# A held weight cast, a sum that starts in PSUM, and the last 384 columns scaled by TensorE: a change to a decoder layer on one core

## The chip, the core and the metric

The kernel runs on one core of a Trainium2 chip. The metric is device time in microseconds (us) of one execution, of which the profiled execution's span is the part between the first and the last recorded instruction.

Engines: PE is TensorE (matrix products), PEld its weight loads, DVE is VectorE, ACT is ScalarE, POOL is GpSimd, SP is SyncE, which here issues nearly all transfers.

## The reference

One decoder layer over 256 tokens of width 1024, batch 1, in float32:

```
z = h @ w_in;  u, q, k, v = split(z)                    # 512 columns each
pool = ((window mean of u) - u) @ w_pool[g] * pool_scale # windows 2, 4, 8, 16, one group of 128 each
attn = softmax(causal(q k^T / 8)) v                     # 8 heads of 64, one block of 256
h = LN1(alpha h + concat(pool, attn) @ w_out)
h = LN2(alpha h + cross_attention(h, mem) @ w_xo)       # 4 heads of 256, 256 memory tokens
h = LN3(alpha h + (silu(h w_gate) * (h w_up)) @ w_down) # d_ff = 2816
```

LN is (x - mean) / sqrt(var + eps) * g + b over the 1024 columns. alpha is 2 to the power 1/4.

## The kernel before

**Precision.** [...] So each operand is split into a high part (a cast by ScalarE) and a low part (the difference, by VectorE), and a product is three: high by high, high by low, low by high (`three`, L325 to L329). Operands that are left plain float32 (`f32`) go through TensorE in two slow passes: the transposes' data, the attention products and the pooled ones (`mix_pool`, L584).

**Weights.** All weights come in one stream (`Stream`, L49 on) of numbered tiles w0 to w130: a raw tile loaded by SP (w26r), then its cast (w26h, L157, ScalarE) and its subtraction (w26l, L159, VectorE). `prepare(upto)` issues casts and subtractions up to a tile, in program order on both engines, and lets SP load on as raw buffers come free (7 of them). Products ask for weights with `get`, which prepares what is needed and, unless `held` is set, one tile more at every `pace`-th call (L175). Instructions stand on each engine in the order in which the program issues them; there is no other scheduler.

**The stretch around the third pair.** After the q, k, v and u projections, the keys of the memory are projected (`xk`, L345, 32 steps of six products, at a pace of 3), and between its steps stand the pieces of the self-attention and the pooling. For each pair of heads, `probs_t(hp)` transposes the probabilities on TensorE into two PSUM banks pt (L543 to L545) and copies them to SBUF: the larger one on VectorE (sb, L548), the smaller on ScalarE (L549). `mix_pool(g)` multiplies the pooled group g by its matrix into a bank pm (L584), and splits the result (L585 ScalarE, L586 VectorE). `pool_diff(g)` (L580, VectorE) makes the input of mix_pool from GpSimd's window sums (L573, L576). Four PSUM banks go around among pt, pm and po (the attention product, L560 and L561); each has to be read out before it is written again. The order is: 12 steps of xk, probs_t(2), mix_pool(0), 8 steps, probs_t(3), mix_pool(1), pool_diff(2), 8 steps, attend(2), mix_pool(2), and so on (L634 on).

**The end.** The down projection of the FFN accumulates the two halves of tokens (t = 0, 1) in eight PSUM banks m; its last six weight tiles (w125 to w130) are multiplied piece by piece (`pieces`, L1034): 512 columns three times, then 256 twice. The very last piece, columns 768 to 1024 of t = 1, has its own bank (acc). Before that, what the other banks hold is joined with the residual in SBUF (r, L1074 to L1084; L1069 adds a bank to r). Each finished piece is added to r (L1069) and measured (L674, bn_stats). Then `finish` runs: aggregate (L679), variance plus eps (L681), power -1/2 on GpSimd (rs, L682), centring, which is (r - mean) * g (L687), scaling, which is r * rs + b (L692), and stores (L991). For t = 0 the scaling is done by ScalarE and GpSimd (L698, L699); for t = 1 it is done by VectorE in pieces of 512, 256 and 256 columns, each stored as soon as it is there.

Of the kernel before, what the change touches and what calls it, by code (L numbers as in the profile page):

```python
# [8 lines left out]
F32 = mybir.dt.float32  # L9
F32R = mybir.dt.float32r  # L10
AF = mybir.ActivationFunctionType
# [3 lines left out]
P = 128  # L15
D = 1024
# [3 lines left out]
CW = 256  # L20
# [13 lines left out]
PR_BUFS = 6  # L34
# [3 lines left out]
DOWN = (1, 0, 2, 3, 4, 7, 5, 6, 8, 9, 10)  # L38
SEVEN = (1, 2, 3, 4, 5, 6)
LAST = DOWN[-3:]  # L40


def r32(t):
    return t.bitcast(F32)


class Stream:
# [115 lines left out]
    def next(self):  # L163

        if not self.held:
            self.prepare(min(self.used + AHEAD, len(self.tiles) + 1))
# [27 lines left out]
def decoder_layer(  # L194
# [17 lines left out]
    def bank(name):  # L212
        return pb.tile([P, 512], F32, tag="b", name=name)

    def accbank(name):
        return pa.tile([P, 512], F32, tag="acc", name=name)


    ws = Stream(nc, wp)
# [70 lines left out]
    gb = {}  # L290
# [14 lines left out]

    ident = cp.tile([P, P], F32, name="ident")
    make_identity(nc, ident)
    tri = ep.tile([P, S], F32, name="tri")
    nc.gpsimd.memset(tri, 0.0)
    nc.gpsimd.affine_select(  # L310
# [13 lines left out]
    def three(ps, w, y, start, stop, part=False):  # L324

        (wa, wb), (ya, yb) = w, y
        nc.tensor.matmul(ps, wa, ya, start=start, stop=False, skip_group_check=part)  # L327
        nc.tensor.matmul(ps, wa, yb, start=False, stop=False, skip_group_check=part)  # L328
        nc.tensor.matmul(ps, wb, ya, start=False, stop=stop, skip_group_check=part)  # L329

    def pair(hl, *ix):
        return hl[0][ix], hl[1][ix]
# [48 lines left out]
    def run(gen, n=None):  # L381

        while n is None or n > 0:
            if next(gen, gen) is gen:
                return False
            n = None if n is None else n - 1
        return True

    def split(h, l, ps):
        nc.scalar.copy(h, ps)  # L390
        nc.vector.tensor_sub(l, ps, r32(h))  # L391
# [146 lines left out]
    def probs_t(hp):  # L538
        p0 = bank("pt0").rearrange("p (j t) -> p j t", j=2)
        p1 = bank("pt1")[:, :S].rearrange("p (j t) -> p j t", j=2)  # L540
        for j in range(2):
            q0, q1 = probs[hp // 2, 0, j][:, hp % 2], probs[hp // 2, 1, j][:, hp % 2]
            nc.tensor.transpose(p0[:, j, :P], q0[:, :P], ident)  # L543
            nc.tensor.transpose(p0[:, j, P:], q1[:, :P], ident)
            nc.tensor.transpose(p1[:, j, :], q1[:, P:], ident)  # L545
        sb = sp.tile([P, 2, 512], F32, name="sb", tag="pair", bufs=3)
        s0, s1 = sb[:, :, :S], sb[:, :, S:S + P]
        nc.vector.tensor_copy(s0, p0)  # L548
        nc.scalar.copy(s1, p1)  # L549
        pts[hp] = s0, s1  # L550
# [31 lines left out]
    def mix_pool(g):  # L582
        pm = bank("pm")
        nc.tensor.matmul(pm[:, :S], pool_w[:, g * P:(g + 1) * P], upad[:, g, PADW:], start=True, stop=True)  # L584
        nc.scalar.activation(cT[0][:, g, :], pm[:, :S], AF.Copy, bias=0.0, scale=psc[:, g:g + 1])  # L585
        nc.vector.scalar_tensor_tensor(cT[1][:, g, :], pm[:, :S], psc[:, g:g + 1],  # L586
                                       r32(cT[0][:, g, :]), op0=OP.mult, op1=OP.subtract)


    def do_v():  # L590
        pieces = [(t, 0, 512) for t in range(T)]
        acc = {piece: accbank("pv") for piece in pieces}
        yield from proj_rows(acc, c_v, lambda k: (xT[0][:, k], xT[1][:, k]), pieces, True, True, True)
        for piece in pieces:
            nc.scalar.copy(vt[:, piece[0], :], acc[piece])

    def do_u():
        for c in range(2):
            ps = accbank("pu").rearrange("p (f t) -> p f t", f=2)
# [6 lines left out]
    def do_xk():  # L606
        for c in range(4):
            ps = accbank("pxk").rearrange("p (f t) -> p f t", f=2)
            yield from proj_t([ps[:, f, :] for f in range(2)], c_xk[c], mT)
            split(xkT[0][:, 2 * c:2 * c + 2, :], xkT[1][:, 2 * c:2 * c + 2, :], ps)  # L610

    v, u, xk = do_v(), do_u(), do_xk()
# [18 lines left out]
    pool_diff(0)  # L631
    pool_diff(1)
    run(u)
    run(xk, 12)  # L634
    probs_t(2)
    mix_pool(0)
    run(xk, 8)
    probs_t(3)
    mix_pool(1)
# [17 lines left out]
    class Norm:  # L657
# [7 lines left out]
        def add(self, c0, c1, acc):  # L665
            self.sum(c0, c1, acc)
            self.measure(c0, c1)
# [2 lines left out]
            s = slice(c0, c1)  # L670
            nc.vector.scalar_tensor_tensor(self.r[:, s], self.tok[:, s], ALPHA, acc, op0=OP.mult, op1=OP.add)

        def measure(self, c0, c1):
            nc.vector.bn_stats(self.st[:, self.n, :], self.r[:, c0:c1])  # L674
            self.n += 1

        def stats(self):
# [3 lines left out]
            nc.vector.tensor_scalar(self.rs, self.mv[:, 1:2], EPS, None, op0=OP.add)  # L681
            nc.gpsimd.tensor_tensor(self.rs, self.rs, mhalf, op=OP.pow)  # L682

        def centre(self, c0, c1):
            s = slice(c0, c1)
            r = self.r[:, s]
            nc.vector.scalar_tensor_tensor(r, r, self.mv[:, 0:1], gb["g", self.i][:, s],  # L687
                                           op0=OP.subtract, op1=OP.mult)

        def scale(self, c0, c1):  # L690
# [10 lines left out]
        def finish(self):  # L701
            self.stats()
            for half in HALVES:
                self.centre(*half)
            for half in HALVES:
                self.scale(*half)

    HALVES = ((0, 512), (512, D))
# [22 lines left out]
    def until(gen):  # L731

        for got in gen:
            if got is not None:
                return got
# [6 lines left out]
    for t in range(T):  # L742
        norm = Norm(1, xt[:, t, :], h1[:, t, :])
# [123 lines left out]
    norm = Norm(2, h1[:, 0, :], h2[:, 0, :])  # L867
# [3 lines left out]
    norm = Norm(2, h1[:, 1, :], h2[:, 1, :])  # L871
# [29 lines left out]
    def gated_pair(c, k, t):  # L901

        return pair(gT[c], ALL, 2 * k + t)
# [86 lines left out]
    def store(t, y, c0, c1, queue=nc.sync):  # L990
        queue.dma_start(out[t * P:(t + 1) * P, c0:c1], y[:, c0:c1])  # L991
# [5 lines left out]
    def into(n, y, w, cols=ALL, ps=None):  # L997

        three((m[n] if ps is None else ps)[:, cols], y, w, n not in begun, True, True)
        begun.add(n)  # L1000
# [32 lines left out]

    def pieces():  # L1034

        for n, c0, c1 in ((2, 0, 512), (3, 0, 512), (4, 0, 512), (0, 0, 256), (0, 256, 512)):
            t, first, _ = QUARTERS[n]
            ps = accbank("acc") if c0 else m[n]
            for c in LAST:
                for k, number in enumerate(c_dn[c]):  # L1040
                    ws.prepare(number + 1)
                    w = pair(ws.tiles[number], ALL, 0, slice(first + c0, first + c1))
                    if c0:
                        three(ps[:, :c1 - c0], gated_pair(c, k, t), w, (c, k) == (LAST[0], 0), True, True)
                    else:
                        into(n, gated_pair(c, k, t), w, slice(c0, c1))
                    yield
            yield ps[:, :c1 - c0] if c0 else ps

    def down():  # L1050
        for c in DOWN[:-len(LAST)]:
            yield from (seven if c in SEVEN else eight)(c)

    dn = down()
# [8 lines left out]
    norms = [Norm(3, h2[:, t, :]) for t in range(T)]  # L1063

    def with_residual(t, s, y):
        nc.vector.scalar_tensor_tensor(norms[t].r[:, s], h2[:, t, s], ALPHA, y, op0=OP.mult, op1=OP.add)
# [15 lines left out]
    nc.vector.tensor_add(norms[1].r[:, upper], norms[1].r[:, upper], u3)  # L1082
    with_residual(1, lower, u3)
    add(norms[1], 768, D, m[0][:, 256:])  # L1084
    dn = pieces()

    def finish(norm, t):

        norm.stats()
        for half in HALVES:  # L1090
            norm.centre(*half)
        if t == 0:
            for half in HALVES:
                norm.scale_apart(*half)
            store(t, norm.r, 0, D)
            return
        for c0, c1, queue in ((0, 512, nc.sync), (512, 768, nc.scalar), (768, D, nc.sync)):
            norm.scale(c0, c1)
            store(t, norm.r, c0, c1, queue)

    norm = norms[0]
    for half in HALVES:
        add(norm, *half, until(dn))
        norm.measure(*half)
    finish(norm, 0)

    norm = norms[1]
    add(norm, *HALVES[0], until(dn))
    norm.measure(*HALVES[0])
    add(norm, 512, 768, until(dn)[:, :256])  # L1110
    norm.measure(512, 768)
    add(norm, 768, D, until(dn))
    norm.measure(768, D)
    finish(norm, 1)
    run(dn)


# [46 lines left out]
```

## Time and profile before

| | us |
|---|---|
| median of 3 runs | 379.49 (379.37 to 379.83) |
| profiled execution | 379.23 |
| its span | 377.5 |
| TensorE busy in the span | 368.3 |
| VectorE, ScalarE, GpSimd busy | 302.3, 201.3, 20.2 |

The lines quoted below come from the profile's page and from views of the trace. A timeline row gives start, duration, engine, source line, operation, output <- inputs, partitions x elements with types, how many; in brackets, how long the engine had been idle and which engine's operation ended that. A row of waits gives engine and operation, what it waited for, us in total, how often, and the longest. A group's row gives busy us and the mean ns of one behind the first bar. A transfer's row ends with its size and the us from issue to landing. A row of windows gives the stretch and its length, each engine's busy us, the granted TensorE clock (1.00 is full), the transfer share and GB/s. A row of the chain gives start, us and what. [...]

### The profile page before, as it was taken

How to read it: one execution, taken by the hardware profiler on the slowest of the kernel's cores; microseconds unless marked ns; L12 is line 12 of the kernel's file. 1: busy time of each engine (PE TensorE's matmuls, PEld its weight loads, DVE VectorE, ACT ScalarE, POOL GpSimd, SP SyncE). 2: the span in 40 equal slices, each digit the busy share in tenths (PEclk: the TensorE clock that was granted, in tenths of full speed). 3: DMA queues.
4: the chain of work that ended last, by engine and by line, in shares of the span. 5: the costliest groups of instructions: out<-in, count | busy, mean ns of one | idle time of the engine just before them, and what ended most of it. 6: DMA issues, size and time to landing. Idle time of an engine off the chain costs nothing.

```text
span 377.5 us, 5729 instructions
## 1 busy us (share of the span) xinstructions
PE 368.3 (98%) x2154; PEld 323.3 (86%) x2154; DVE 302.3 (80%) x470; ACT 201.3 (53%) x318; POOL 20.2 (5%) x27
## 2 busy tenths in 40 slices
PE   9999999899999999999999999999999999999992
PEld 8997989798888889998888888888888888888882
DVE  6868889955499687774899687788876998999995
ACT  5746668543253544644237575556666466466510
POOL 1000036100020000000100000000000000000022
PEclk9999999999999999999999999999999999999997
DMA  7997773658606964343206854666555863363102
GB/s 282 412 413 259 219 281 115 220 171 283 214 6 236 411 203 143 123 128 121 87 0 226 310 186 175 220 222 198 168 175 163 302 224 112 109 206 132 56 2 111
DMA packets 20892, 71.95 MB, mean 191 GB/s; under 512 B 2304, under 2 KB 3072, under 8 KB 20736
## 3 DMA queue, kind: packets, MB, share of 16 engines
q1 hardware_dynamic: 20432, 71.18, 54.3%
q8 instruction: 17, 0.28, 0.3%
q10 hardware_dynamic: 432, 0.39, 0.3%
q14 instruction: 11, 0.09, 0.1%
HBM read 70.52 MB, written 1.05 MB: 190 GB/s over the span
## 4 chain that ended last, share of the span: by engine, by line
PE 93%; DVE 2%; issue 2%; ACT 1%; DVEq 0%; ACTq 0%
PE pg L780 19%; PE pg L786 10%; PE pqk L461 6%; PE m L328 5%; PE m L329 5%; PE m L327 5%; PE pxk L345 4%; PE acc L327 4%; PE acc L328 4%; PE acc L329 4%; PE pxq L780 4%; PE pxq L786 2%; PE xv L327 2%; PE xv L329 2%; PE xv L328 2%
## 5 line engine op out<-in xcount | busy, mean ns | idle before, releaser
L682 POOL TENSOR_TENSOR rs<-rs,mhalf 128x1 f32<-128x1 f32 x6 | 5.4, 892 | 296.2 <-DVE rs L681 296.2
L390 ACT CAST g<-sg 128x512 fp32r<-128x512 f32 x12 | 7.4, 621 | 15.1 <-DVE sg L954 10.1
L391 DVE TENSOR_TENSOR g<-sg,g 128x512 fp32r<-128x512 f32 x12 | 8.3, 693 | 8.2 <-ACT g L390 8.2
L935 DVE TENSOR_TENSOR sg<-pg,sg 128x256 f32<-128x256 f32 x40 | 14.1, 416 | 0.0
L934 ACT COPY sg<-pg 128x256 f32<-128x256 f32 x40 | 12.0, 386 | 3.5 <-PE pg L786 3.3
L939 ACT ACTIVATE sg<-sg 128x512 f32<-128x512 f32 x10 | 6.4, 635 | 13.8 <-DVE sg L935 13.8
L497 ACT ACTIVATE xpr<-xs,mx 128x256 f32<-128x256 f32 x8 | 3.7, 468 | 14.3 <-DVE mx L508 14.3
L497 ACT ACTIVATE pr<-pr,mx 128x128 f32<-128x128 f32 (+1 forms) x16 | 7.1, 444 | 7.2 <-DVE mx L528 7.2
L390 ACT CAST h2T<-tp 128x512 fp32r<-128x512 f32 x4 | 2.3, 587 | 13.0 <-PE tp L418 12.9
L674 DVE BATCH_NORM_STATS2 st<-r 128x6 f32<-128x512 f32 (+1 forms) x13 | 8.5, 654 | 0.5
L687 DVE SCALAR_TENSOR_TENSOR r<-r,mv,g 128x512 f32<-128x512 f32 x12 | 8.5, 743 | 0.0
L940 DVE TENSOR_TENSOR sg<-sg 128x512 f32<-128x512 f32 x10 | 6.9, 692 | 0.9
L698 ACT ACTIVATE r<-r,rs 128x512 f32<-128x512 f32 x2 | 1.3, 716 | 11.4 <-POOL rs L682 11.4
L502 DVE RECIPROCAL sm<-sm 128x2 f32<-128x2 f32 x12 | 2.0, 166 | 6.0 <-ACT xpr L497 4.5
L812 PE MATMUL xs<-xkTh,xq 128*128 128x256 f32 x32 | 6.4, 282 | 0.0
L390 ACT CAST h1T<-tp 128x512 fp32r<-128x512 f32 x4 | 2.3, 587 | 7.1 <-PE tp L418 7.1
L573 POOL TENSOR_TENSOR win<-upad 128x542 f32<-128x542 f32 x2 | 3.2, 1596 | 54.4 <-ACT upad L601 54.4
L692 DVE SCALAR_TENSOR_TENSOR h<-r,rs,b 128x512 f32<-128x512 f32 x8 | 5.7, 747 | 0.1
L812 PEld LDWEIGHTS xs<-xkTh,xq 128*128 128x128 f32 x32 | 5.2, 191 | 0.2
L573 POOL TENSOR_TENSOR win<-win 128x269 f32<-128x269 f32 (+3 forms) x4 | 5.2, 1307 | 0.2
L157 ACT CAST w39h<-w39r 128x1024 fp32r<-128x1024 f32 x1 | 1.1, 1060 | 7.8 <-PE acc L329 7.8
L390 ACT CAST xkTh<-pxk 128x512 fp32r<-128x512 f32 x4 | 2.4, 588 | 4.9 <-PE pxk L345 4.9
(1169 smaller groups left out, 1376.7 us busy)
## 6 DMA issues: line engine op xcount, KB each, us to landing
g<-in_ln_g SPq DMA_DIRECT2D x3, 512.0 KB, 5.8
b<-in_ln_b SPq DMA_DIRECT2D x3, 512.0 KB, 6.8
wr<-in_w_qkv SPq DMA_DIRECT2D x5, 256.0 KB, 4.0
mr<-in_mem_t SPq DMA_DIRECT2D x1, 1024.0 KB, 11.3
xt<-in_x SPq DMA_DIRECT2D x1, 1024.0 KB, 8.5
xr<-in_x_t SPq DMA_DIRECT2D x3, 256.0 KB, 6.4
wr<-in_w_qkv SPq DMA_DIRECT2D x1, 512.0 KB, 6.2
w7r<-in_w_qkv SPq DMA_DIRECT2D x1, 512.0 KB, 7.2
```

The source lines that it names most:

```text
L327: nc.tensor.matmul(ps, wa, ya, start=start, stop=False, skip_group_check=part)
L328: nc.tensor.matmul(ps, wa, yb, start=False, stop=False, skip_group_check=part)
L329: nc.tensor.matmul(ps, wb, ya, start=False, stop=stop, skip_group_check=part)
L345: nc.tensor.matmul(pss[f], w[:, s], y, start=k == 0 and f == 0 and n == 0, stop=k == KD - 1 and n == 2, skip_group_check=True)
L390: nc.scalar.copy(h, ps)
L461: nc.tensor.matmul(qk[i][:, f, :], w[:, c * P:(c + 1) * P], y, start=k == 0 and f == 0 and w is hi and y is x_hi, stop=k == KD - 1 and w i ...
L497: nc.scalar.activation(dst[:, j, :], src[:, j, :], AF.Exp, bias=mx[:, j:j + 1], scale=sign, accum_out=sm[:, j:j + 1])
L780: nc.tensor.matmul(ps, hi[:, b * P:(b + 1) * P], yT.both(k), start=k == 0, stop=False, skip_group_check=True)
L786: nc.tensor.matmul(ps[:, S:], lo[:, b * P:(b + 1) * P], yT.pair(k)[0], start=False, stop=k == KD - 1, skip_group_check=True)
L812: nc.tensor.matmul(ps[:, t, :], q[:, kk, t * P:(t + 1) * P], k[:, 2 * h + kk], start=n == 0, stop=q is q_lo and kk == 1, skip_group_check= ...
L934: nc.scalar.copy(y[:, f, :], ps[:, S:])
L935: nc.vector.tensor_add(y[:, f, :], ps[:, :S], y[:, f, :])
```

## The change

Three edits, with a copy of the identity matrix in fp32r (ident_r) made at the start by VectorE.

1. After 7 of the 12 steps of xk ahead of the third pair's probs_t(2), the stream is held: no weight is prepared ahead until probs_t(2) and mix_pool(0) have been issued.
2. The last piece (columns 768 to 1024 of t = 1) does not begin with zero. What r already holds there is split into a high and a low part (rest), and two products with ident_r put it into the bank acc first. The addition afterwards goes; statistics and centring read acc directly.
3. Of the last norm's scaling, columns 640 to 1024 are done by TensorE: a product of the identity with b (128x384, float32), then one of a diagonal matrix of rs (made by ScalarE) with the centred r, summed in a bank, which ScalarE copies to SBUF and stores. VectorE scales columns 0 to 512 and 512 to 640. The centring goes in the order 768 to 1024, 640 to 768, 0 to 640. The stores are 512 columns (SP), 384 (ScalarE's queue) and 128 (SP), instead of 512, 256, 256.

```
+CUT = 640
...
+    ident_r = cp.tile([P, P], F32R, name="ident_r")
+    nc.vector.tensor_copy(ident_r, ident)
...
-    run(xk, 12)
+    run(xk, 7)
+    ws.held = True
+    run(xk, 5)
     probs_t(2)
     mix_pool(0)
+    ws.held = False
     run(xk, 8)
...
-        def measure(self, c0, c1):
-            nc.vector.bn_stats(self.st[:, self.n, :], self.r[:, c0:c1])
+        def measure(self, c0, c1, src=None):
+            nc.vector.bn_stats(self.st[:, self.n, :], self.r[:, c0:c1] if src is None else src)
...
-            nc.vector.scalar_tensor_tensor(r, r, self.mv[:, 0:1], gb["g", self.i][:, s],
+            nc.vector.scalar_tensor_tensor(r, r if src is None else src, self.mv[:, 0:1], gb["g", self.i][:, s],
...
             ps = accbank("acc") if c0 else m[n]
+            for part in rest if c0 else ():
+                nc.tensor.matmul(ps[:, :c1 - c0], ident_r, part, start=part is rest[0], stop=False,
+                                 skip_group_check=True)
...
-                        three(ps[:, :c1 - c0], gated_pair(c, k, t), w, (c, k) == (LAST[0], 0), True, True)
+                        three(ps[:, :c1 - c0], gated_pair(c, k, t), w, False, True, True)
...
     add(norms[1], 768, D, m[0][:, 256:])
+    rest = [sp.tile([P, CW], F32R, name=f"rest{i}", tag="pr", bufs=PR_BUFS) for i in range(2)]
+    split(*rest, norms[1].r[:, 768:])
     dn = pieces()
...
-    add(norm, 768, D, until(dn))
-    norm.measure(768, D)
-    finish(norm, 1)
+    acc = until(dn)
+    norm.measure(768, D, acc)
+    norm.stats()
+    norm.centre(768, D, acc)
+    norm.centre(CUT, 768)
+    norm.centre(0, CUT)
+    diag = sp.tile([P, P], F32, name="diag", tag="pr", bufs=PR_BUFS)
+    nc.scalar.activation(diag, ident, AF.Copy, bias=0.0, scale=norm.rs)
+    ps = bank("end")[:, :D - CUT]
+    nc.tensor.matmul(ps, ident, gb["b", 3][:, CUT:], start=True, stop=False)
+    nc.tensor.matmul(ps, diag, norm.r[:, CUT:], start=False, stop=True)
+    norm.scale(0, 512)
+    store(1, norm.r, 0, 512)
+    nc.scalar.copy(norm.r[:, CUT:], ps)
+    store(1, norm.r, CUT, D, nc.scalar)
+    norm.scale(512, CUT)
+    store(1, norm.r, 512, CUT)
     run(dn)
```

On each engine's list of instructions the first edit moves one weight: w26's cast goes from ahead of the smaller copy of probs_t(2) to behind the xk cast, and its subtraction from ahead of the copy sb to behind the xk subtraction; w27 to w30 each follow one place later, and from w31 on the lists agree again up to the end.

More of the change, by code (lines that the diff above doesn't have):

```diff
@@ L682, in stats, with centre @@
             nc.gpsimd.tensor_tensor(self.rs, self.rs, mhalf, op=OP.pow)
-        def centre(self, c0, c1):
+        def centre(self, c0, c1, src=None):
             s = slice(c0, c1)
             r = self.r[:, s]
-            nc.vector.scalar_tensor_tensor(r, r, self.mv[:, 0:1], gb["g", self.i][:, s],
+            nc.vector.scalar_tensor_tensor(r, r if src is None else src, self.mv[:, 0:1], gb["g", self.i][:, s],
                                            op0=OP.subtract, op1=OP.mult)
@@ L1084, in decoder_layer @@
     add(norms[1], 768, D, m[0][:, 256:])
+    rest = [sp.tile([P, CW], F32R, name=f"rest{i}", tag="pr", bufs=PR_BUFS) for i in range(2)]
+    split(*rest, norms[1].r[:, 768:])
     dn = pieces()
[L1087 to L1099, printed above, removed]
     norm = norms[0]
@@ L1104, in decoder_layer @@
         norm.measure(*half)
-    finish(norm, 0)
+    norm.stats()
+    for half in HALVES:
+        norm.centre(*half)
+    for half in HALVES:
+        norm.scale_apart(*half)
+    store(0, norm.r, 0, D)
     norm = norms[1]
@@ L1111, in decoder_layer @@
     norm.measure(512, 768)
-    add(norm, 768, D, until(dn))
-    norm.measure(768, D)
-    finish(norm, 1)
+    acc = until(dn)
+    norm.measure(768, D, acc)
+    norm.stats()
+    norm.centre(768, D, acc)
[12 more added lines that the diff above has]
+    store(1, norm.r, 512, CUT)
     run(dn)
```

## The prediction

> **What bounds the kernel now.** I read the page's head first, then the waits of TensorE, then the timeline at each place that the change touches.
>
> ```profile
> span 377.5 us, 5729 instructions
> PE 368.3 (98%) x2154; PEld 323.3 (86%) x2154; DVE 302.3 (80%) x470; ACT 201.3 (53%) x318; POOL 20.2 (5%) x27
> PE pm L584 <- DVE sb L548: 1.2, 1, 1.2
> ```
>
> TensorE (PE) works 98% of the span. The rest, 377.5 - 368.3 = 9.2 us, has three parts: the one wait of 1.2 us that the list of TensorE's waits gives for its whole run after the start, 7.2 us after its last product (which ends at 370.32, below), and the 0.8 that are left at the start. The change goes at the second and the third. The profiled execution took 379.23 us, 1.73 more than its span; the median of the runs shown is 379.49, so 0.26 above it. About 0.2% (0.76 us) is what a measurement of this kernel can tell from no change.
>
> **1. The cast moved behind the third pair (L634 to L638).** The timeline at that place:
>
> ```profile
> 61.74 3.96 POOL L573 TENSOR_TENSOR win<-win 128x538 f32<-128x538 f32 x2
> 61.87 0.27 PE L544 MATMUL pt<-ident,pr 128*128 128x128 f32 x1
> 61.98 0.27 PE L545 MATMUL pt<-ident,pr 128*128 128x128 f32 x1
> 62.64 0.28 PE L345 MATMUL pxk<-mTl,w20h 128*128 128x256 f32 x1
> 62.67 2.10 DVE L159 TENSOR_TENSOR w25l<-w25r,w25h 128x1024 fp32r<-128x1024 f32 x1
> 64.69 2.09 DVE L159 TENSOR_TENSOR w26l<-w26r,w26h 128x1024 fp32r<-128x1024 f32 x1
> 65.94 0.27 PE L545 MATMUL pt<-ident,pr 128*128 128x128 f32 x1
> 66.71 0.68 DVE L548 COPY sb<-pt 128x512 f32<-128x512 f32 x1
> 67.44 0.70 PE L584 MATMUL pm<-upad,pool_w 128*128 128x256 f32 x2 [1.24 <-DVE sb L548]
> 68.10 0.28 PE L345 MATMUL pxk<-mTl,w21h 128*128 128x256 f32 x1
> ```
>
> The transposes of the third pair end at 62.25, but VectorE (DVE) copies them only at 66.71: w25l and w26l stand ahead of it. The product of mix_pool(1) at 67.44 needs the PSUM bank that this copy frees, so TensorE stands still. The same sequence, without the wait, stands three rows into the fence: from the last transpose to the second product behind the pooled one it takes 62.64 - 61.98 = 0.66 us. With the wait it takes 68.10 - 65.94 = 2.16. The wait costs 1.50 us, the start after it included.
>
> In the changed program's order only w26's cast and subtraction leave their place (the pace of three lets one through in the five steps that are held); they go behind the copy, the pooled subtraction and the xk one. So the copy can start at 64.69, when w25l is done, and end at 65.4, over 0.5 us ahead of 65.94. The wait goes wholly: **-1.50**. What is late next has to be looked for on VectorE:
>
> ```profile
> 67.31 0.47 DVE L586 SCALAR_TENSOR_TENSOR cTl<-pm,pool_w,cTh 128x256 fp32r<-128x256 f32 x1
> 67.70 0.68 DVE L391 TENSOR_TENSOR xkTl<-pxk,xkTh 128x512 fp32r<-128x512 f32 x1
> 68.30 1.21 DVE L159 TENSOR_TENSOR w27l<-w27r,w27h 128x1024 fp32r<-128x1024 f32 x1
> 70.43 0.41 DVE L580 SCALAR_TENSOR_TENSOR upad<-win,upad 128x256 f32<-128x256 f32 x1
> 71.74 0.70 PE L584 MATMUL pm<-upad,pool_w 128*128 128x256 f32 x2
> 83.78 0.28 PE L345 MATMUL pxk<-mTh,w26h 128*128 128x256 f32 x1
> 83.86 1.05 ACT L157 CAST w33h<-w33r 128x1024 fp32r<-128x1024 f32 x1 [1.23 <-PE pxk L345]
> 289.15 1.22 DVE L159 TENSOR_TENSOR w99l<-w99r,w99h 128x1024 fp32r<-128x1024 f32 x1 [2.98 <-PE pg L786]
> ```
>
> mix_pool(2) would now come at 71.74 - 1.50 = 70.24, and needs pool_diff(2), the L580. Before, w26l and w27l stood ahead of that; now w26l alone, since w27l goes behind it. From 64.69: copy, L586 and xkTl (0.68, 0.47, 0.68) to 66.5; w26l, between 1.21 (GpSimd still) and 2.09 (GpSimd adding), to 67.7 or 68.6; copy and L586 to 69.7; L580 to 70.1 at the worst. That is in time by 0.1 to 1.0 us. w26 to w30, whose splits come later, are used from 83.78 on. The load that waits for w26l's raw buffer (w33, seven buffers on, in SP's queue) and those behind it start up to 1.8 us later; w33 is cast at 83.86 only. Does the gain last to the end? TensorE waits nowhere after 68, and VectorE was itself waiting for TensorE as late as w99l at 289 (2.98 us), so its work moves along.
>
> **2. The sum by TensorE, then the last norm.** The rows of the end:
>
> ```profile
> 370.07 0.12 PE acc L328
> 370.34 0.42 DVE L1069 TENSOR_TENSOR r<-acc,r 128x256 f32<-128x256 f32 x1 [1.27 <-PE acc L329]
> 370.80 0.43 DVE L674 BATCH_NORM_STATS2 st<-r 128x6 f32<-128x256 f32 x1
> 371.26 0.24 DVE L679 BATCH_NORM_AGGREGATE mv<-st 128x2 f32<-128x18 f32 x1
> 371.53 0.15 DVE L681 TENSOR_SCALAR rs<-mv 128x1 f32<-128x1 f32 x1
> 371.60 1.40 DVE L687 SCALAR_TENSOR_TENSOR r<-r,mv,g 128x512 f32<-128x512 f32 x2
> 371.83 0.92 POOL L682 TENSOR_TENSOR rs<-rs,mhalf 128x1 f32<-128x1 f32 x1 [2.46 <-DVE rs L681]
> 372.93 1.54 DVE L692 SCALAR_TENSOR_TENSOR r<-r,rs,b 128x512 f32<-128x512 f32 x3
> 373.70 1.12 SPq L991 DMA_DIRECT2D out<-r  x2
> out<-r ACTq DMA_DIRECT2D x1, 128.0 KB, 2.1
> ```
>
> (All times of this part are in the old clock, without the 1.50.) Two more products of 256 columns, 0.12 each, put the end of TensorE's sum 0.24 later. The addition goes, a step of 370.80 - 370.34 = 0.46. So the measuring starts at 370.58 instead of 370.80: 0.22 earlier. I take the statistics from PSUM at the same 0.43, since the addition reads PSUM in 0.42. Then the power (rs) on GpSimd ends at 372.53 instead of 372.75.
>
> From there TensorE's way is new. Its rows are found elsewhere:
>
> ```profile
> L497 ACT ACTIVATE pr<-pr,mx 128x128 f32<-128x128 f32 x8 | 3.1, 391 | 3.3 <-DVE mx L528 3.3
> L934 ACT COPY sg<-pg 128x256 f32<-128x256 f32 x40 | 12.0, 386 | 3.5 <-PE pg L786 3.3
> L390 ACT CAST h2T<-tp 128x512 fp32r<-128x512 f32 x4 | 2.3, 587 | 13.0 <-PE tp L418 12.9
> 68.18 0.47 ACT L585 ACTIVATE cTh<-pm,pool_w 128x256 fp32r<-128x256 f32 x1 [1.51 <-PE pm L584]
> ```
>
> The diagonal, 128x128 on ScalarE: between 0.39 (the exponential with its sum) and 0.29 (the copies of 512 and 256, carried on to 128); 0.33 and a hand-off of 0.03 bring 372.89. A plain float32 product of 256 columns took 67.39 (copy done) to 68.18 (ScalarE starts on it): 0.79. For 384 columns two passes of 128 more are added; a pass of 128 costs 0.11 (61.87 to 61.98), so 1.01, to 373.90. ScalarE copies 384 columns in the mean of 386 and 587 ns, 0.49, to 374.39. Its store is issued at 374.43 and lands 2.1 us later.
>
> VectorE's part is shorter: centring 256, 128 and 640 columns (0.42, 0.28, 0.80 by the steps of 0.66 for 512 and 0.43 for 256) ends at 372.88; scaling 512 and 128 columns to 373.85. SP's second store goes out at about 374.0, not at 373.70 + 1.12 - 0.34 = 374.48 as before. So the last store is ScalarE's: 374.43 against 374.48, **-0.05**. Bounds: diagonal and copy at their cheapest -0.2; all hand-offs at 0.1 more each +0.3. The product of the identity with the shift waits for nothing late and lies in the 1.7 us in which TensorE is idle anyway.
>
> **3. What is hidden.**
>
> ```profile
> 3.21 0.29 DVE L483 CAST xTh<-xr 128x256 fp32r<-128x256 f32 x1 [0.15 <-DMA xr<-in_x_t]
> 361.42 1.01 DVE L1069 TENSOR_TENSOR r<-m,r 128x256 f32<-128x256 f32 x2
> 368.19 0.42 DVE L1069 TENSOR_TENSOR r<-m,r 128x256 f32<-128x256 f32 x1 [0.62 <-PE m L329]
> ```
>
> The copy of the identity goes ahead of VectorE's first work; the 0.15 us for which it waited for data cover it nearly (0 to 0.1 if not, and TensorE is then still at its warming products). The split of rest puts a ScalarE cast (0.39, as the copy of 256) and a subtraction (0.42) into VectorE's row at 361.8, about 0.87 with the hand-offs. Of that, 0.62 is taken up at 368.19 and the remaining 0.25 by the 1.27 of waiting at 370.34. The first half's store goes out 0.87 later, at about 370.3, long before the last ones.
>
> **Sum.** -1.50 - 0.05 = -1.55: 379.23 becomes 377.68, and the median 379.49 becomes **377.9**.
>
> **The clock.** The new diagonal product is the first in this kernel that follows a pause of TensorE late in the run.
>
> ```profile
> 372.90:373.00 0.10, 0.00 (x0) 0.00 (x0) 0.10 (x2) 0.00 (x0) 0.00 (x0) 0.80 0.00 0
> 0.77 3.33 PE busy L431 x14
> ```
>
> The granted clock is 0.80 on the mean of this tenth, so it fell from 1.00 to 0.50 at about 372.96, 2.64 us after the last product ended at 370.32. In the changed kernel the shift's product ends near 371.2 and the diagonal's starts at 372.9, a pause of 1.7 us, 0.9 shorter. If the clock has fallen by then, the product's three groups of 128 columns at 0.11, in two passes (0.66), double: +0.66; by the first products of the run, 3.33/14 = 0.24 for a pass of 128 instead of 0.11, +0.78.
> [...]
>
> **The rivals.**
> (a) The clock falls before or in the diagonal's product: 377.9 + 0.66 to 0.78, about 378.6. For it: it did fall within 2.64 us. Against it: the pause is shorter, and the shift's product lies in it. 0.13.
> (b) The wait goes only in part: the copy is slowed beside GpSimd's additions (as w24l to w26l are, 2.1 for 1.21), or pool_diff(2) comes up to 0.6 late. Gain about 0.9: 378.6. Against it: the copy read PSUM in 0.68 while GpSimd was adding. 0.10.
> (c) The hold does nothing for TensorE, because its wait simply becomes one on another operation of the same length; the end alone is left: 379.4. 0.05.
> (d) Slower: the wait takes its place at mix_pool(2), behind w26l. TensorE is at 70.24 there, and the change becomes slower than 0.2% if pool_diff(2) ends later than 71.74 + 0.05 + 0.76 = 72.55, against the 70.1 of my worst case. That takes 2.4 us more on VectorE, more than w26l's whole 2.09 once again; with two such delays it would be 380.2. Against it: GpSimd has less to wait for, as VectorE's three operations ahead of w26l read PSUM. 0.04.
> (e) The forecast: 0.68.
>
> **How the numbers follow.** Forecast with its own bounds (-0.2 to +0.3): 377.6 to 378.2, widened by 0.1 for the spread of runs to 377.5 to 378.3. The range takes in (a) and (b): 377.5 to 378.8, leaving out (c), (d) and a tenth of the forecast. Faster by over 0.2% (below 378.73): all of (e), and most of (a) and (b): 0.87. Within 0.2%: (c), the rest of (a) and (b): 0.09. Slower: 0.04.
>
> **What would show it.** Right: no wait of pm on sb in TensorE's list, the L548 copy ending before the next pair's transposes, TensorE's first stretch unbroken to the sum's end at about 370.3 + 0.24 - 1.50 = 369.1; the ScalarE store as the last, about 4.1 us behind that. Wrong: a new wait of TensorE between 66 and 76 us, on pool_diff or a bank; a granted clock of 0.50 at the diagonal's product; a ScalarE copy that starts more than 1.2 us behind the diagonal; VectorE late for the last sum, with no wait ahead of its statistics.

## The result, and the profile after

The changed kernel took 378.10 us (median of 6 runs, 377.68 to 378.59), against 379.72 for the kernel before (6 runs, 379.37 to 380.28). The ratio is 0.9957, with a 95% interval of 0.9944 to 0.9970. That is 1.62 us faster; the forecast was 1.55 us, 377.9 for a median before of 379.49. Three executions that took 459 us or more (one each of hold_only, hold_early and one_store below) are left out of all times and ratios, and since it was the profiled one in hold_only and hold_early, no trace of these two is read.

The page's head of the changed kernel, and a row of TensorE's waits (us in total, how often, the longest):

```profile
span 376.4 us, 5745 instructions
PE 370.3 (98%) x2160; PEld 324.5 (86%) x2160; DVE 301.4 (80%) x471; ACT 202.7 (54%) x321; POOL 19.8 (5%) x27
PE end L1128 <- ACT diag L1125: 1.5, 1, 1.5
```

The wait of 1.2 us of pm on sb is gone from the list. In its place stands one of 1.5 us ahead of the diagonal's product; it lies behind the last product of the sum, in time in which TensorE was idle before as well. The lines have moved: L584 is now L588, L548 is L552, L159 is L161, L580 is L584.

The timeline at the third pair, on both engines:

```profile
62.46 0.27 PE L549 MATMUL pt<-ident,pr 128*128 128x128 f32 x1
63.15 2.10 DVE L161 TENSOR_TENSOR w25l<-w25r,w25h 128x1024 fp32r<-128x1024 f32 x1
65.17 0.68 DVE L552 COPY sb<-pt 128x512 f32<-128x512 f32 x1
66.42 0.27 PE L549 MATMUL pt<-ident,pr 128*128 128x128 f32 x1
66.77 1.49 DVE L161 TENSOR_TENSOR w26l<-w26r,w26h 128x1024 fp32r<-128x1024 f32 x1
67.08 0.28 PE L349 MATMUL pxk<-mTl,w21h 128*128 128x256 f32 x1
69.17 0.41 DVE L584 SCALAR_TENSOR_TENSOR upad<-win,upad 128x256 f32<-128x256 f32 x1
70.73 0.48 PE L588 MATMUL pm<-upad,pool_w 128*128 128x256 f32 x1
```

The copy starts when w25l is done, at 65.17, and is over (65.85) before the transposes that end at 66.69. From the last of these to the second product behind the pooled one it takes 67.08 - 66.42 = 0.66 us, where it took 2.16: 1.50 less. w26l now stands behind the copy, and pool_diff(2) (L584) still ends at 69.58, 1.15 us ahead of the product that needs it at 70.73.

The whole timeline stands 0.48 us later here than in before (62.46 for 61.98). That comes from the start: by the traces' records of the granted clock, TensorE's went to full at 5.63, where it did at 4.32 in before. The same pair of its first products took, in before and then in the changed kernel:

```profile
4.33 0.40 PE L461 MATMUL pqk<-xTl,w0h 128*128 128x256 f32 x2
```

```profile
4.32 0.63 PE L465 MATMUL pqk<-xTl,w0h 128*128 128x256 f32 x2
```

This is why the two spans differ by only 1.08 us (377.46 and 376.38). So I measure in two stretches that don't contain the start: the middle, from the last transpose ahead of the place of the wait (65.94 in before) to the start of the sum's last product (370.02), and the end, from there to the end of the span. The middle took 304.08 before and 302.77 now, -1.31, though it contains two more products (0.24). The end took 7.44 and 7.19, -0.25. Together -1.56.

The timeline of the end, with SP's and ScalarE's stores, and what the last two stores took to land:

```profile
369.19 0.28 PE L333 MATMUL acc<-w130h,go 128*128 128x256 f32 x1
369.51 0.43 DVE L681 BATCH_NORM_STATS2 st<-acc 128x6 f32<-128x256 f32 x1 [1.28 <-PE acc L333]
370.32 0.48 DVE L694 SCALAR_TENSOR_TENSOR r<-acc,mv,g 128x256 f32<-128x256 f32 x1
370.55 0.55 POOL L689 TENSOR_TENSOR rs<-rs,mhalf 128x1 f32<-128x1 f32 x1 [1.32 <-DVE rs L688]
370.71 1.14 DVE L694 SCALAR_TENSOR_TENSOR r<-r,mv,g 128x128 f32<-128x128 f32 x2
371.13 0.40 ACT L1125 ACTIVATE diag<-ident,rs 128x128 f32<-128x128 f32 x1 [3.90 <-POOL rs L689]
371.58 0.91 PE L1128 MATMUL end<-r,diag 128*128 128x384 f32 x2 [1.46 <-ACT diag L1125]
371.95 1.01 DVE L699 SCALAR_TENSOR_TENSOR r<-r,rs,b 128x512 f32<-128x512 f32 x2
372.53 0.48 ACT L1131 COPY r<-end 128x384 f32<-128x384 f32 x1 [1.00 <-PE end L1128]
373.04 0.39 ACTq L998 DMA_DIRECT2D out<-r  x1
373.17 0.38 SPq L998 DMA_DIRECT2D out<-r  x1
```

```profile
out<-r ACTq DMA_DIRECT2D x1, 192.0 KB, 2.3
out<-r SPq DMA_DIRECT2D x1, 64.0 KB, 2.4
```

The statistics start 0.32 behind the last product's start, where the added r made it 0.78. The power (L689) took 0.55, not the 0.92 of before. The diagonal's product follows 1.46 us of idle time and ran at the full clock (1.00 from 371 to 373). The last store to land is SP's of 64 KB, at 373.17 + 2.4 = 375.6; ScalarE's lands at 373.04 + 2.3 = 375.3.

### The profile page after: what moved, and what is told of

Its sections match the earlier page's. It is cut to its first block, busy times and chain, and to the rows that moved or that the text cites. A ratio compares the mean times of both kernels' runs of the same rounds, so it can differ in the third digit from the quotient of the medians.

```text
span 376.4 us, 5745 instructions
## 1 busy us (share of the span) xinstructions
PE 370.3 (98%) x2160; PEld 324.5 (86%) x2160; DVE 301.4 (80%) x471; ACT 202.7 (54%) x321; POOL 19.8 (5%) x27
## 4 chain that ended last, share of the span: by engine, by line
PE 98%; ACT 0%; DVE 0%; POOLq 0%; issue 0%
PE pg L787 19%; PE pg L793 10%; PE pqk L465 6%; PE pxk L349 6%; PE m L332 5%; PE m L331 5%; PE m L333 5%; PE acc L331 4%; PE acc L332 4%; PE acc L333 4%; PE pxq L787 4%; PE pu L349 3%; PE pxq L793 2%; PE xv L333 2%; PE xv L331 2%; PE xv L332 2%
## 5 line engine op out<-in xcount | busy, mean ns | idle before, releaser
L689 POOL TENSOR_TENSOR rs<-rs,mhalf 128x1 f32<-128x1 f32 x6 | 5.0, 830 | 294.4 <-DVE rs L688 294.4
L694 DVE SCALAR_TENSOR_TENSOR r<-r,mv,g 128x512 f32<-128x512 f32 (+2 forms) x12 | 8.3, 722 | 0.0
L159 ACT CAST w39h<-w39r 128x1024 fp32r<-128x1024 f32 x1 | 1.1, 1056 | 7.8 <-PE acc L333 7.8
L395 DVE TENSOR_TENSOR h1T<-tp,h1T 128x512 fp32r<-128x512 f32 x4 | 2.8, 690 | 2.7 <-ACT h1T L394 2.7
```

## The experiments

The theory: the hold alone makes the gain; the end is worth nothing net, since what the shorter chain gives, the two products take. The main rival: the end carries the gain, or the gain is the start's phase. hold_only ran again as hold_again for its trace. The table collects all runs; each ratio is to executions of before taken beside that run; wait is that of pm on sb, and middle and end are the two stretches above.

| kernel | time, us | ratio to before, 95% | wait | middle | end |
|---|---|---|---|---|---|
| before | 379.72 | | 1.2 | 304.08 | 7.44 |
| changed | 378.10 | 0.9957 (0.9944 to 0.9970) | none | 302.77 | 7.19 |
| hold_only | 378.13 | 0.9955 (0.9942 to 0.9969) | | | |
| hold_again | 377.80 | 0.9956 (0.9943 to 0.9968) | none | 302.57 | 7.43 |
| end_only | 379.48 | 0.9998 (0.9989 to 1.0007) | 1.2 | 304.30 | 7.19 |
| rest_only | 379.90 | 1.0003 (0.9994 to 1.0012) | 1.2 | 304.31 | 7.30 |
| scale_only | 380.14 | 1.0010 (1.0001 to 1.0018) | 1.2 | 304.09 | 7.78 |
| hold_early | 378.41 | 0.9962 (0.9949 to 0.9976) | | | |
| one_more | 381.51 | 1.0049 (1.0035 to 1.0063) | 2.4 | 306.97 | 7.43 |
| one_more_again | 382.22 | 1.0064 (1.0046 to 1.0081) | 2.4 | 306.92 | 7.43 |
| windows_late | 379.69 | 1.0001 (0.9993 to 1.0010) | 1.2 | 304.08 | 7.42 |
| no_windows | 378.46 | 0.9961 (0.9949 to 0.9973) | none | 302.57 | 7.42 |
| sbuf_first | 377.92 | 0.9953 (0.9941 to 0.9966) | none | 302.80 | 7.17 |
| one_store | 378.11 | 0.9963 (0.9950 to 0.9976) | none | 302.83 | 7.39 |

**The parts of the change.** hold_only and hold_again are before with the hold:

```
-    run(xk, 12)
+    run(xk, 7)
+    ws.held = True
+    run(xk, 5)
     probs_t(2)
     mix_pool(0)
+    ws.held = False
```

> The kernel before with the hold alone (no casts of the later weights ahead of the third pair's transposed probabilities); the final addition, scaling and stores are those of before. Theory: the whole gain is the removed wait. TensorE shows no wait of about 1.5 us on the evacuation of the transposed probabilities in the third pair, the time is 1.5 us below before (ratio about 0.996), and from the start of the last product of the sum to the end of the span it takes 7.4 us as before. Rival 1, the end carries the gain: the wait goes but comes back elsewhere, and the time is within 0.3 us of before. Rival 2, the gain is only a different phase of the clock's start: then the spans with the start of the transposes of the third pair's probabilities as zero differ by under 0.5 us.

> The hold alone once more, for its trace. Theory: no wait in the third pair, and 7.4 us from the start of the sum's last product to the end of the span as before, against 7.2 in the changed kernel with its two further products (0.24) ahead of that: the same time as the changed kernel within 0.3 us. Rival, the end of the changed kernel is worth something by itself: the hold alone is 0.5 us or more above it.

The hold by itself gives the time of the whole change, and the middle is 1.51 us shorter than in before, with the end as before (7.43). In its trace the copy, the last transpose and the product behind the pooled one stand as in the changed kernel:

```profile
64.78 0.68 DVE L548 COPY sb<-pt 128x512 f32<-128x512 f32 x1
66.02 0.27 PE L545 MATMUL pt<-ident,pr 128*128 128x128 f32 x1
66.68 0.28 PE L345 MATMUL pxk<-mTl,w21h 128*128 128x256 f32 x1
```

Again 66.68 - 66.02 = 0.66. The last transpose stands within 0.08 of before's (65.94), so here the start's phase has no part in it. Both rivals fall.

end_only is the changed kernel without the hold:

```
-    run(xk, 7)
-    ws.held = True
-    run(xk, 5)
+    run(xk, 12)
     probs_t(2)
     mix_pool(0)
-    ws.held = False
```

> The changed kernel without the hold: only the sum that begins with what there is of it, and TensorE's scaling of the last 384 columns. Theory: the end is worth nothing net (forecast -0.05; two more products +0.24, the chain behind the last product shorter by about as much), so the time is that of before within 0.3 us, TensorE's wait of 1.2 to 1.5 us in the third pair is still there, and from the start of the last product of the sum to the end it takes 7.2 us where before takes 7.44. Rival, the end carries the gain: 1 us or more below before.

```profile
PE pm L588 <- DVE sb L552: 1.2, 1, 1.2
```

That row is its list of waits: the wait is there again. The middle is 0.22 longer by the two products, the end 0.25 shorter, and the time is that of before. Theory borne out.

rest_only takes only the sum's start from the change, scale_only only TensorE's scaling. Their diffs against before, cut to what differs:

```
+            for part in rest if c0 else ():
+                nc.tensor.matmul(ps[:, :c1 - c0], ident_r, part, start=part is rest[0], stop=False,
+                                 skip_group_check=True)
...
+    acc = until(dn)
+    norm.measure(768, D, acc)
+    norm.stats()
+    norm.centre(768, D, acc)
+    norm.centre(512, 768)
+    norm.centre(0, 512)
...
```

```
     add(norm, 768, D, until(dn))
     norm.measure(768, D)
+    norm.stats()
+    norm.centre(768, D)
+    norm.centre(CUT, 768)
+    norm.centre(0, CUT)
...
```

In the first, VectorE scales and stores columns 0 to 512, 512 to 768 and 768 to 1024, as before; in the second, the diagonal, its products, the copy and the stores are those of the change.

> The kernel before with the start of the last sum in PSUM alone (identity copy, two products of it, no addition behind the sum); VectorE scales all columns, stores of 512, 256 and 256 columns. Theory that GpSimd's power is short when VectorE beside it reads PSUM: the power takes 0.55 us and not 0.92, and the statistics start 0.46 earlier against the last product; with +0.24 for the two products the time is 0.2 to 0.6 us below before. Rival, the power's length has nothing to do with what VectorE reads: 0.92 us, and the gain is 0.2 or less.

> The kernel before with TensorE's scaling of the last 384 columns alone; the addition stays and the statistics and the centring read SBUF. Theory: the diagonal on ScalarE (0.4), its product (0.9 to 1.0) and the copy (0.5) end later than VectorE's scaling of the same columns would, and the power takes 0.92 as before: the store behind the product goes out 0.4 to 0.5 us later against the last product of the sum than in the changed kernel, and the time is 0.0 to 0.4 us above before. Rival, TensorE's scaling is what gains at the end: 0.3 us or more below before.

rest_only: the power took 0.55, as the first theory has it, but the time did not fall. Its timeline shows where the 0.46 of the missing addition went:

```profile
371.69 0.48 DVE L691 SCALAR_TENSOR_TENSOR r<-acc,mv,g 128x256 f32<-128x256 f32 x1
371.91 0.55 POOL L686 TENSOR_TENSOR rs<-rs,mhalf 128x1 f32<-128x1 f32 x1 [1.29 <-DVE rs L685]
372.08 1.14 DVE L691 SCALAR_TENSOR_TENSOR r<-r,mv,g 128x256 f32<-128x256 f32 x2
373.32 1.54 DVE L696 SCALAR_TENSOR_TENSOR r<-r,rs,b 128x512 f32<-128x512 f32 x3
```

VectorE's scaling waits for its own centring, not for the power, which is ready at 372.46. The columns 0 to 512, which are scaled first, are now centred last, so the scaling starts 0.10 after the centring's end (373.22), where in before it started 0.07 ahead of it (372.93 against 373.00). With a third centring instruction (1.53 us from first to last, for 1.40) this takes back 0.3 of the 0.46; the end is 0.14 shorter, and the two products cost 0.23.

scale_only: the addition stays, so the diagonal's chain starts late:

```profile
372.08 0.66 POOL L684 TENSOR_TENSOR rs<-rs,mhalf 128x1 f32<-128x1 f32 x1 [2.48 <-DVE rs L683]
374.74 0.37 ACTq L993 DMA_DIRECT2D out<-r  x1
```

ScalarE's store goes out 374.74 - 370.27 = 4.47 behind the start of the last product, against 3.85 in the changed kernel: 0.62 later, where 0.4 to 0.5 was expected. The end is 0.34 longer than before's. The power took 0.66 and not 0.92, so the expected price of reading SBUF was off; what its length went with is below. Of the 0.62, the addition is 0.46 and the longer power 0.10. The last 0.06 is the clock: its mean is 0.97 from 373.00 to 374.00 and 0.50 after that, so it fell at 373.94, inside the diagonal's product (373.22 to 374.19). What the prediction's rival (a) describes did happen here. TensorE's scaling pays only together with the sum that is measured in PSUM, and even then only what the two products cost.

**How much one weight is worth.** hold_early is the changed kernel with the hold after 4 steps in place of 7, one_more is the kernel before with w27 prepared ahead of the third pair:

```
-    run(xk, 7)
+    run(xk, 4)
     ws.held = True
-    run(xk, 5)
+    run(xk, 8)
```

```
     run(xk, 12)
+    ws.prepare(len(ws.tiles) + 1)
     probs_t(2)
```

> The changed kernel with the hold from the fourth step of the piece before on instead of the seventh, so that one more weight (w25) waits until the third pair's probabilities are transposed. Theory: TensorE's wait is already gone with the smaller hold, and the weights that come later still come in time, so the time is that of the changed kernel within 0.3 us, and TensorE shows no new wait. Rival, each weight that is held is worth something by itself: 0.5 us or more below the changed kernel. Rival, the held weights run late: a new TensorE wait between 66 and 76 us, 0.5 us or more above it.

> The kernel before with one weight more (w27) prepared ahead of the third pair's transposed probabilities. Theory: VectorE's copy of the transposed probabilities stands behind the low parts of the weights in its queue, so each further one adds its own length (1.2 to 2.1 us) to TensorE's wait of 1.2 us; the wait is 2.4 to 3.3 us and the time 1.2 to 2.1 us above before. Rival, the wait is set by something other than that queue (the transposes' own bank, ScalarE): the wait stays at 1.2 us and the time within 0.3 us of before.

hold_early gains no more than the changed kernel, so it is the wait that is worth something and not each weight. one_more is 1.86 us slower than before by its ratio (0.0049 of 379.62). VectorE's two instructions and the pooled product:

```profile
66.87 1.24 DVE L159 TENSOR_TENSOR w27l<-w27r,w27h 128x1024 fp32r<-128x1024 f32 x1
68.03 0.68 DVE L548 COPY sb<-pt 128x512 f32<-128x512 f32 x1
68.76 0.48 PE L584 MATMUL pm<-upad,pool_w 128*128 128x256 f32 x1 [2.39 <-DVE sb L548]
```

The wait grew from 1.24 to 2.39, by the 1.16 us that w27l holds the queue. But the middle grew by 2.89. The rest is the clock, in the windows (the column before the last two is the granted clock):

```profile
70.00:70.20 0.20, 0.20 (x4) 0.20 (x3) 0.20 (x1) 0.00 (x0) 0.00 (x0) 0.86 2.26 246
73.40:73.60 0.20, 0.20 (x3) 0.20 (x2) 0.00 (x0) 0.00 (x0) 0.00 (x0) 0.60 0.44 164
```

A mean of 0.86 over 0.20 us puts the fall to one half at 70.14, and 0.60 the rise at 73.56: 3.41 us at half the clock, a loss of 1.7. With 1.15 of wait that is 2.85 of the 2.89. I ran it again to see whether the fall belongs to the pause:

> The kernel before with one weight more (w27) ahead of the third pair's transposed probabilities, once more, to see a second trace: the first showed a wait of 2.4 us and, from 1.4 us behind it, half the clock for 3.41 us. Theory that the clock is decided in windows of 3.41 us whose place differs from run to run: the wait is 2.4 us again, but the half-clock stretch begins at another place against the wait or is not there, and the span without it is 1.2 us above before. Rival, the fall belongs to the pause by its length: half the clock for 3.4 us again at 1.4 us behind the wait, and 1.7 us of loss with it.

```profile
68.00:69.00 1.00, 0.24 (x1) 0.24 (x2) 1.00 (x3) 0.00 (x0) 0.91 (x2) 0.73 0.93 250
71.00:72.00 1.00, 1.00 (x7) 1.00 (x6) 1.00 (x3) 0.00 (x0) 0.00 (x0) 0.57 0.82 328
```

The wait is 2.4 again, but the clock falls at 68.46, still within the pause, and rises at 71.86. The place moved by 1.7 us against the same pause and the length stayed, so the rival, a fixed delay behind the pause, falls. Of the nine executions of this kernel four took 381.36 to 381.57 and five 382.22 to 382.48. Both traces are of the upper five. No trace shows the other four, but the times do: with the wait and the fall, 2.85 us together, none could be below 382.0, since the fastest execution of before on record took 379.15. So these four escaped the fall, at least in part.

**Why the copy was late.** The subtractions w24l to w26l took 2.1 us each in before, w27l 1.2. The theory is GpSimd's window sums beside them.

```
-            windows(c)
+            if c == 0:
+                windows(c)
...
     mix_pool(0)
+    windows(1)
```

> The kernel before, with the second pair's pooling windows on GpSimd issued behind the first mix of the pool instead of ahead of it, and no hold. Theory that GpSimd's additions draw out VectorE's subtractions: w24l to w26l take 1.2 us each and not 2.1, the copy of the third pair's transposed probabilities comes up to 2.6 us earlier, and TensorE's wait of 1.2 us on it is gone: 1.5 us below before, as long as the windows are still in time for the pool's difference (70.2 us); if they come late, there is a new wait on it. Rival, the subtractions are long for another reason: they stay at 2.1 us, the wait stays at 1.2 us, the time within 0.3 us of before.

The edit moved nothing on the chip: GpSimd has its own queue, waits there for upad alone, and began as early as before, in this row of its timeline:

```profile
60.19 1.56 POOL L573 TENSOR_TENSOR win<-upad 128x542 f32<-128x542 f32 x1 [5.20 <-ACT upad L601]
```

So it tells nothing of the theory. no_windows leaves these sums out:

```
+        if c == 1:
+            sums[2], sums[3] = upad[:, 2, :], upad[:, 3, :]
+            return
```

> The kernel before without GpSimd's window sums of the second pair of groups (left out: the pool's difference of these two groups takes the group itself in place of its sum), and no hold. Theory that GpSimd's additions draw out VectorE's subtractions and so cause the wait: w24l to w26l take 1.2 us each and not 2.1, the copy of the third pair's transposed probabilities comes up to 2.6 us earlier, TensorE's wait of 1.2 us on it is gone, and the time is 1.5 us below before, as with the hold. Rival, the subtractions are long for another reason (the DMAs that write SBUF beside them): they stay at 2.1 us, the wait stays at 1.2 us, and the time is within 0.3 us of before.

```profile
61.38 1.22 DVE L159 TENSOR_TENSOR w24l<-w24r,w24h 128x1024 fp32r<-128x1024 f32 x1
64.79 0.68 DVE L548 COPY sb<-pt 128x512 f32<-128x512 f32 x1
66.68 0.27 PE L545 MATMUL pt<-ident,pr 128*128 128x128 f32 x1
```

All three subtractions stand ahead of the copy, as in before, but at 1.22 each (w24l's row; w25l and w26l the same) the copy comes at 64.79, 1.9 us ahead of the last transpose, and the wait is gone: the middle is 302.57, to the hundredth that of the hold. The wait has two conditions, and either one's removal takes all of it: w26's subtraction ahead of the copy, and GpSimd's sums beside the subtractions.

**The end.** sbuf_first turns the order of the centring, one_store joins SP's last two stores:

```
+    norm.centre(0, CUT)
     norm.centre(768, D, acc)
     norm.centre(CUT, 768)
-    norm.centre(0, CUT)
```

```
-    norm.scale(0, 512)
-    store(1, norm.r, 0, 512)
+    norm.scale(0, CUT)
+    store(1, norm.r, 0, CUT)
...
-    norm.scale(512, CUT)
-    store(1, norm.r, 512, CUT)
```

> The changed kernel with the order of VectorE's centring turned: columns 0 to 640 (read from SBUF) first, then 768 to 1024 (from PSUM), then 640 to 768. Theory that GpSimd's power can't run beside a centring from SBUF and starts when that ends: the power ends about 0.45 us behind the end of the first centring (640 columns, about 0.85 us), so its span is 1.0 to 1.1 us where the changed kernel has 0.55; diagonal, product and copy come 0.5 us later against the last product of the sum, ScalarE's store becomes the last, and the time is 0.2 to 0.4 us above the changed kernel. Rival, the power's length is its own: 0.55 us, and the chain ends as in the changed kernel.

> The changed kernel with VectorE scaling columns 0 to 640 in one instruction and one SP store of them (320 KB) in place of two (256 and 64 KB). Theory that the last 64 KB store, behind SP's other and beside ScalarE's, is what lands last (issued at 373.2, landed 2.4 later): with it gone, ScalarE's store (373.0, 2.3 or less) lands last, and from the start of the sum's last product to the end of the span it takes 0.1 to 0.3 us less than the changed kernel's 7.19; the time is 0.0 to 0.3 us below the changed kernel's. Rival, the bytes and not the issues set the landing: the larger store, issued some 0.3 us later than the first of the two, lands last itself, and the end is the same or up to 0.3 us longer.

sbuf_first, its timeline and ScalarE's store:

```profile
370.30 0.88 DVE L694 SCALAR_TENSOR_TENSOR r<-r,mv,g 128x640 f32<-128x640 f32 x1
370.53 1.06 POOL L689 TENSOR_TENSOR rs<-rs,mhalf 128x1 f32<-128x1 f32 x1 [1.32 <-DVE rs L688]
371.75 1.01 DVE L699 SCALAR_TENSOR_TENSOR r<-r,rs,b 128x512 f32<-128x512 f32 x2
373.53 0.35 ACTq L998 DMA_DIRECT2D out<-r  x1
```

```profile
out<-r ACTq DMA_DIRECT2D x1, 192.0 KB, 1.9
```

The power is as long as the theory said, 1.06, and ScalarE's store goes out 0.49 later. But the time is the changed kernel's. The scaling starts 0.20 earlier, because the columns that it needs first are centred first, and the two last stores no longer land side by side: ScalarE's took 1.9 and lands at 375.4, where the changed kernel's last landed at 375.6. The step from a later issue to a later end was wrong.

one_store: SP's one store lands early enough, but ScalarE's takes longer beside it:

```profile
372.62 0.34 SPq L998 DMA_DIRECT2D out<-r  x1
372.79 0.36 ACTq L998 DMA_DIRECT2D out<-r  x1
```

```profile
out<-r SPq DMA_DIRECT2D x1, 320.0 KB, 2.2
out<-r ACTq DMA_DIRECT2D x1, 192.0 KB, 2.6
```

ScalarE's is the last now (372.79 + 2.6 = 375.4, SP's at 374.8), as the theory said, but it gained nothing: the end is 7.39, 0.20 longer. That is within the rival's range, but not for the rival's reason, since SP's larger store does not land last. No run beats the changed kernel by more than the measurement tells; the hold alone is as fast.

## Why the prediction was right, point by point

**Part 1, -1.50.** Shown. The hold alone shortens the middle by 1.51, and the sequence behind the last transpose goes from 2.16 to 0.66. The copy starts at 65.17, which is the predicted 64.69 and the 0.48 of the later start. "That is in time by 0.1 to 1.0 us" was slightly low: pool_diff(2) had 1.15 us to spare, since GpSimd was nearly done and w26l took 1.49. So (b), (c) and (d) did not happen.

**Two more products, +0.24.** Measured +0.22 and +0.23 in end_only and rest_only.

**The end, -0.05 with the two products.** Measured +0.24 - 0.25, about zero, but by other terms. "Then the power (rs) on GpSimd ends at 372.53" kept 0.92; it took 0.55, and TensorE's chain was 0.37 shorter for it. The diagonal took 0.40 and not 0.33; from its end to the copy's start went 1.00, against 1.01. So ScalarE's store came 3.53 behind the start of the statistics (373.04 - 369.51), not 3.85. The step that failed is "So the last store is ScalarE's": SP's last store came 3.66 behind the statistics, not 3.42, of which 0.10 is the gap between the centring's end and the scaling, where I had none, and the rest small differences in centring, scaling and issue; and it landed in 2.4, not 2.1. SP's 64 KB took the place that I gave to ScalarE's 192 KB, and the sum for the end came out by luck, by errors of opposite sign.

**What is hidden.** The copy of the identity (at 1.34, 0.30 us; VectorE then still stands idle for 0.41 us up to 2.06, where its next work started in before as well) and the split of rest cost nothing:

```profile
361.28 0.43 DVE L395 TENSOR_TENSOR rest<-r,rest 128x256 fp32r<-128x256 f32 x1 [0.53 <-ACT rest L394]
```

That row of the changed kernel's timeline is the split's subtraction. Behind it, the statistics still waited 1.28 for the last product, as long as the addition did in before.

**The clock, (a).** It did not fall ahead of the diagonal's product. A row of the changed kernel's windows puts the fall behind it:

```profile
374.00:375.00 1.00, 0.00 (x0) 0.00 (x0) 0.00 (x0) 0.00 (x0) 0.00 (x0) 0.63 0.96 352
```

The second before it has 1.00, so a mean of 0.63 puts the fall at 374.26, 1.8 us after the product's end at 372.49. The rival was priced by the pause's length alone; in the traces the falls went with how much of one clock window of 3.41 us (last section) TensorE stood idle. They came behind windows with 2.02 us idle or more, in scale_only with a pause of 2.02 us ahead of the diagonal's product. The changed kernel's pause was 1.46 us, and end_only had 1.63 us idle in one window without a fall. So with this pause the rival was out of reach wherever the windows lay, as far as these traces show.

## What to carry to other kernels

Where TensorE waits for a PSUM bank, look at what stands ahead of the copy in the copying engine's queue, and move the work that nobody needs yet: 1.5 us of a 98% busy TensorE came back for no instruction saved. A wait of two causes can be taken away at either, so find out which is cheaper to move. At the end of this kernel, an instruction saved on one chain was worth only what the other chain and the landing of the last stores left of it (in rest_only 0.46 us saved made the end 0.14 shorter); work these out side by side, with their order of columns.

## What the runs showed of the hardware

**The clock's windows.** By the traces' own records of the granted clock, the stretch at full clock is 368.64 us long in before (4.32 to 372.96) and in the changed kernel (5.63 to 374.26). The stretch at half in one_more (70.14 to 73.56) is 3.41 us, and 368.64 / 108 = 3.4133. The other stretches at full clock that were read, 372.05 in end_only, 64.85 and 303.79 in one_more, are 109, 19 and 89 times 3.4133. So in these traces the end of the full clock is tied to its start, and the phase at the start moves both. That the clock is decided window by window, in windows of 3.41 us, is my reading of these multiples. Idle time in a window went with a fall only where there was enough of it: the window ahead of one_more's fall at 70.14 (from 66.73) held 2.03 us of pause, 59% of it, the one ahead of one_more_again's at 68.46 held 2.09, 61%, and the one ahead of scale_only's 373.94 held 2.02, 59%. The pause of 1.24 us in before, 36% of a window, caused no fall. In end_only the window from 370.50 to 373.91 held 1.63 us without a product, 48% (1.46 ahead of the diagonal's product and the rest behind it), and the clock stayed full, as these rows of its timeline and its windows show:

```profile
372.83 0.91 PE L1125 MATMUL end<-r,diag 128*128 128x384 f32 x2 [1.46 <-ACT diag L1122]
375.00:376.00 1.00, 0.00 (x0) 0.00 (x0) 0.00 (x0) 0.00 (x0) 0.00 (x0) 1.00 1.01 380
```

The clock fell at 377.33, behind a window that was wholly idle. So by these traces the limit lies between 48% and 59% of a window; where, no run shows.

**The power beside VectorE.** GpSimd's power of 128 numbers ended 0.41 us after the end of VectorE's first centring where that reads both inputs from SBUF: 371.59 behind 371.18 in sbuf_first, 372.75 behind 372.34 in before (two of 512 columns in 1.40, started 0.66 apart, so 0.74 each), and 372.74 behind 372.33 in scale_only. Where the centring reads PSUM, it took 0.55 and ended 0.30 behind it. The subtractions, which read both inputs from SBUF, took 2.10 us beside GpSimd's sums and 1.22 without them (no_windows). In before, GpSimd's product of 128x16 took 1.08 us beside w26l (at 65.78) and 0.22 beside cTl and xkTl, which read PSUM banks (at 67.63). What makes the difference was not shown.

**Stores side by side.** A store of 192 KB landed in 1.9 us when the store of 64 KB had gone out 0.57 ahead of it, in 2.3 with that 0.13 behind, and in 2.6 beside one of 320 KB. What makes the difference was not measured.

**Steps and passes.** A matmul's record is longer than the step to the next start, so steps are read here from the differences of starts. In before, fp32r products of 256 columns stand as one record of 0.28 us each, 0.12 apart (60.11, 60.23). The pooled plain float32 product of 256 columns stands as two records of 0.38, 0.22 apart (62.09, 62.31). A plain float32 transpose of 128 columns stands as one record of 0.27, 0.11 apart from the next (61.87, 61.98), so two passes show for that product and not for the transposes.
